# Delta heads: pairwise decays from spread rows of running sums and a minimum, in place of masked copies summed by products

## The chip, the core and the metric

The kernel runs on one core of a Trainium2 chip. A core has a matrix engine (TensorE; PE in the profile, its weight loads PEld), three engines for element work (VectorE, DVE; ScalarE, ACT; GpSimd, POOL) and SyncE (SP), whose queue issues nearly all transfers between the device memory and the on-chip memories. Each engine works through its own list of instructions in a fixed order; an instruction that waits for a semaphore holds up everything behind it on that engine. The metric is the device time of one execution in microseconds (us), the median of several runs.

## What is computed

One layer of a bidirectional encoder trunk over 1024 tokens of width 1024, in float32: a combined input projection, then in parallel a windowed softmax attention and a bidirectional gated delta rule ("delta heads"), an output projection, a cross-attention into 256 memory tokens, and a feed-forward block. The change lies in the delta heads. There are 4 heads and 2 directions; the tokens are cut into chunks, and inside a chunk every pair of tokens has a decay:

```python
g = -exp(a_log) * softplus(a + dt_bias)          # per token, direction and head; negative
g = cumsum(g, within the chunk)
decay = exp(where(i >= j, g[i] - g[j], -inf))    # c x c per chunk, head and direction
lower = where(i > j, (k*beta) @ k.T * decay, 0)  # solved against v and k
qk    = (q @ k.T) * decay
```

The backward direction is the same on reversed tokens. The kernel works with chunks of 128 tokens, 8 of them (NT), and keeps one 128 x 128 table E per chunk and head that serves both directions: above the diagonal it holds the forward decay, below it the backward one. The key products `k.T k` and the query products `k.T q` are multiplied by it.

## The kernel before

The work runs in stages. The first, some 0 to 230 us of the span, normalises x, transposes it and projects it into the q, k and v of the delta heads (`proj`, `gemm_b`, L276: 48 matrix products of 128x128 by 128x512 for each of 12 column tiles, since every float32 operand is split into a high and a low part and three of the four partial products are summed). Beside the projections run a short convolution with SiLU for each tile (`conv`: copies on ScalarE at L298 and L299, four multiply-adds on VectorE at L301, SiLU on ScalarE at L302) and the preparation of the delta heads. The table `ORDER_1` names the steps of this stage in the order in which they are written: `k0 k1 E0 K0 U0 E1 K1 U1 S0 q0 v0 q1 C0 v1 E2 C1 k2 ...`, where a digit is the head. The steps that matter here:

- E, `decays` (L479 ff.): makes the tables E of one head, in two halves of four chunks each.
- K, `turned_keys`: transposes the keys (L459), copies them (L503) and sums their squares (L467, one pass of 128 columns each).
- U, `key_products`: products of keys (L474) into a PSUM bank, times E (L513).
- S, `beta_rows`: one transpose (L450) of a small tile, stored to device memory and read back by `base_inverse`.
- C, `query_products`: products of queries (L474), times E (L521), masked for each direction (L524); then transposes of queries and values (L459).
- B, `base_inverse`: a triangular inverse in 31 small steps on VectorE (L560, L562).

All PSUM tiles of these steps come from one pool of 5 banks (`small()`), so a transpose or a product can start only when an earlier tile of the pool has been read. In `decays` before, the exponent is summed by TensorE. For each half of a head, the per-token logs g are multiplied with a triangular mask into four 128x512 tiles `gm` (two directions, each in a high and a low part, `ghi` and `glo`), and four products with the strict triangles `mU_r`, `mL_r` (L492) add them up in one PSUM bank. The exponential (L495) reads that bank. VectorE makes the masked copies of heads 0 and 1 (L488), ScalarE those of heads 2 and 3 (L491). Nothing in this step goes through device memory.

After the first stage come the remaining levels of the inverse, the window attention and its projections (`ORDER_2`, 230 to 350 us, with `rr` tiles of the pool `ra` for the rotary part), the scan over chunks (`ORDER_3`), and then the output projection, cross-attention and feed-forward, in which the change touches nothing.

The order on each engine isn't the written one: a scheduler with priorities lays the steps out on the engines when the program is built, and fixes there which buffer and which bank each step takes. Weight loads, their casts (L103) and remainders (L104) are written 300 places ahead. A change in one step thus moves others.

## Time and profile before

| what | value |
|---|---|
| time of the runs, median (lowest, highest of 3) | 1501.22 us (1501.08, 1502.55) |
| span of the profiled execution, first to last instruction | 1497.9 us |
| median of the runs less that span | 3.3 us |
| busy in the span: PE, PEld, DVE, ACT, POOL | 98%, 83%, 74%, 52%, 25% |
| mean granted TensorE clock | 0.995 of full speed |
| all tables E made: first masked copy, last exponential | 67.3 us, 170.8 us |

The page has no time for the profiled execution beside its span; the 3.3 us to the median are taken as the part of a run that lies around the span. The row of the page with a share of 98% for PE says how long products were in flight, not that TensorE ran at its peak. Of each line that a view shows, the first numbers are start and duration (in the timeline), or the count and the mean of one (in groups). "idle before" is time in which that engine had nothing to run, and names whom it waited for. Line numbers are those of the kernel before, unless the text says otherwise; in the changed kernel the lines of the first stage are 2 to 7 lower (L457, L472, L499, L465, L509 for L459, L474, L503, L467, L513).

### The profile page before, as it was taken

What the parts mean: (1) busy time and instruction counts of PE and PEld (TensorE: products, weight loads), DVE (VectorE), ACT (ScalarE), POOL (GpSimd) and SP (SyncE); (2) the same over time, 40 slices, a digit from 0 to 9 for tenths busy, and PEclk for the clock granted to TensorE, in tenths of its full rate; (3) what the DMA queues carried; (4) which work ended last, traced back from release to release, by engine and by line L of the source; (5) the groups of instructions that cost most, each with busy time, mean ns of one, the idle gap of its engine ahead of it and who ended that gap; (6) DMA issues with size and microseconds to landing.
All of it is one profiled execution on the core that took longest, in us unless ns stands there. A gap on an engine that the chain in (4) does not pass through costs nothing.

```text
span 1497.9 us, 21340 instructions
## 1 busy us (share of the span) xinstructions
PE 1467.6 (98%) x7437; PEld 1239.1 (83%) x7437; DVE 1108.8 (74%) x1804; ACT 776.3 (52%) x1600; POOL 374.3 (25%) x411
## 2 busy tenths in 40 slices
PE   7999999999999999999999999999999999999998
PEld 6888878888999878888888877888888888888787
DVE  5878998577897866538767887686867774795666
ACT  7678844568567664555554774323223232544533
POOL 0011232442246213342201002343433342000030
PEclk9999999999999999999999999999999999999999
DMA  6244554657996585444855553343533433953355
GB/s 205 71 120 137 142 168 135 168 173 222 297 305 211 158 310 204 163 146 157 277 174 194 183 197 119 121 141 105 168 123 113 138 109 103 351 183 99 105 181 170
DMA packets 254169, 256.35 MB, mean 171 GB/s; under 512 B 18129, under 2 KB 186222, under 8 KB 254062
## 3 DMA queue, kind: packets, MB, share of 16 engines
q1 hardware_dynamic: 252141, 250.80, 52.7%
q0 software_dynamic: 768, 2.10, 0.5%
q10 hardware_dynamic: 1152, 2.10, 0.4%
q8 instruction: 58, 0.95, 0.3%
q14 instruction: 50, 0.40, 0.1%
HBM read 178.63 MB, written 73.70 MB: 168 GB/s over the span
## 4 chain that ended last, share of the span: by engine, by line
PE 73%; DVE 9%; ACT 4%; issue 2%; DMA 2%; SPq 1%; POOL 0%; DVEq 0%; ACTq 0%
PE pE L1511 8%; PE pD L1511 8%; PE pA L1511 6%; PE pmg L1105 6%; PE pcq L276 6%; PE pdX L1733 6%; PE pst L1324 5%; PE pdA L1733 4%; PE pB L1511 4%; PE pg L276 3%; PE psc L844 3%; PE pdD L1733 2%; PE pdX L1842 2%; PE pcs L1195 2%; PE pco L1222 1%
## 5 line engine op out<-in xcount | busy, mean ns | idle before, releaser
L103 ACT CAST whi<-wraw 128x1024 fp32r<-128x1024 f32 x96 | 100.7, 1050 | 119.5 <-DMA wraw<-in_w_gate_up_dram 40.0
L276 PE MATMUL pg<-hlo,whi 128*128 128x512 f32 x352 | 140.5, 399 | 0.0
L276 PE MATMUL pg<-hhi,whi 128*128 128x512 f32 x352 | 139.6, 396 | 0.0
L276 PE MATMUL pg<-hhi,wlo 128*128 128x512 f32 x352 | 139.2, 395 | 0.0
L104 POOL TENSOR_TENSOR wlo<-wraw,whi 128x1024 fp32r<-128x1024 f32 x37 | 90.3, 2440 | 191.1 <-ACT whi L103 179.1
L1511 PE MATMUL pA<-b,whi 128*128 128x512 f32 x352 | 109.7, 393 | 1.9 <-ACT whi L103 1.0
L104 DVE TENSOR_TENSOR wlo<-wraw,whi 128x1024 fp32r<-128x1024 f32 x59 | 72.5, 1228 | 31.1 <-ACT whi L103 27.0
L1511 PEld LDWEIGHTS pA<-b,whi 128*128 128x128 f32 x352 | 65.3, 188 | 17.1 <-ACT whi L103 1.9
L276 PEld LDWEIGHTS pg<-hhi,whi 128*128 128x128 f32 x352 | 66.6, 189 | 13.5 <-ACT hhi L241 0.3
L276 PEld LDWEIGHTS pg<-hlo,whi 128*128 128x128 f32 x352 | 66.8, 190 | 12.6
L276 PEld LDWEIGHTS pg<-hhi,wlo 128*128 128x128 f32 x352 | 66.8, 190 | 12.4
L1733 PE MATMUL pdX<-dhl,whi 128*128 128x512 f32 x264 | 76.1, 390 | 0.9 <-ACT dhl L103 0.7
L1603 POOL TENSOR_TENSOR act<-act,up 128x512 f32<-128x512 f32 x33 | 50.3, 1524 | 88.6 <-DVE up L1602 67.3
L103 ACT CAST whi<-araw 128x1024 fp32r<-128x1024 f32 (+1 forms) x36 | 35.3, 981 | 68.2 <-PE pdX L1733 27.6
L1511 PE MATMUL pA<-b,wlo 128*128 128x512 f32 x176 | 69.0, 392 | 0.5 <-DVE wlo L104 0.5
L104 DVE TENSOR_TENSOR wlo<-araw,whi 128x1024 fp32r<-128x1024 f32 (+1 forms) x36 | 40.8, 1132 | 33.6 <-ACT whi L103 33.5
L1574 POOL TENSOR_TENSOR sr<-wraw 128x512 f32<-128x512 f32 x22 | 30.0, 1363 | 139.1 <-DMA wraw<-in_w_gate_up_dram 87.1
L301 DVE SCALAR_TENSOR_TENSOR acc<-cp,cols,acc 128x1024 f32<-128x1024 f32 x48 | 63.1, 1316 | 0.2
L1733 PEld LDWEIGHTS pdX<-dhl,whi 128*128 128x128 f32 x264 | 49.3, 188 | 12.1 <-ACT dhl L103 1.1
L103 ACT CAST dhl<-b 128x512 fp32r<-128x512 f32 x66 | 40.3, 620 | 31.3 <-PE pdA L1733 13.5
L1575 DVE TENSOR_TENSOR sr<-sr,wraw 128x512 f32<-128x512 f32 x22 | 36.7, 1666 | 26.2 <-POOL sr L1574 26.2
L103 ACT CAST s0h<-sr 128x512 fp32r<-128x512 f32 x22 | 13.7, 622 | 79.1 <-POOL sr L1574 78.8
(504 smaller groups left out, 4331.5 us busy)
## 6 DMA issues: line engine op xcount, KB each, us to landing
wraw<-in_w_gate_up_dram SPq DMA_DIRECT2D x54, 512.0 KB, 3.9
kv<-d_kv SPq DMA_DIRECT2D x32, 512.0 KB, 6.0
wraw<-in_w_in_dram SPq DMA_DIRECT2D x22, 512.0 KB, 4.1
b<-in_w_down_dram SPq DMA_DIRECT2D x20, 512.0 KB, 6.3
araw<-d_as SPq DMA_DIRECT2D x20, 512.0 KB, 3.6
pz<-d_pz SPq DMA_DIRECT2D x32, 256.0 KB, 6.3
wraw<-in_w_ckv_dram SPq DMA_DIRECT2D x16, 512.0 KB, 5.0
wraw<-in_w_out_dram SPq DMA_DIRECT2D x16, 512.0 KB, 5.4
```

The source lines that it names most:

```text
L103: nc.scalar.copy(hi, src)
L104: return (eng or nc.vector).tensor_tensor(lo, src, f32(hi), ALU.subtract)
L276: nc.tensor.matmul(p_, w[:, k, :], ah[a][:, k, :], start=(k == 0 and i == 0), stop=(k == nk - 1 and i == 2))
L301: nc.vector.scalar_tensor_tensor(acc, cp[:, t:t + S], taps[t], acc, ALU.mult, ALU.add)
L844: nc.tensor.matmul(out[:, d, h, :], lt[:, d, h, :], rt[:, d, h, :], start=True, stop=True)
L1105: nc.tensor.matmul(pp[t], act[a][:, k, tt], w_[:, kk, :], start=(k == 0 and i == 0), stop=(k == KT - 1 and i == 2))
L1324: nc.tensor.matmul(bank, a[:, tt], w, start=(start and i == 0), stop=(stop and i == 2), skip_group_check=not check)
L1511: nc.tensor.matmul(out_, w[a][:, k, :], xx[b_][:, k, :], start=(start and k == 0 and i == 0), stop=(k == HK - 1 and i == 2), skip_group_ch ...
L1574: nc.gpsimd.tensor_tensor(s[0], b_[:, 0:HK], b_[:, HK:], ALU.add)
L1575: nc.vector.tensor_tensor(s[1], s[0], a_[:, 0:HK], ALU.subtract)
L1603: nc.gpsimd.tensor_tensor(o_, o_, up, ALU.mult)
L1733: nc.tensor.matmul(banks[t], a[:, k - k0, tt], w, start=(first and k == 0 and i == 0), stop=(k == NB - 1 and i == 2), skip_group_check=not ...
```

## The change

`decays` no longer uses TensorE. The kernel already computed the inclusive running sums of g within a chunk, forward and backward, by a product with triangles (L385), for the small factors EG. The change copies these sums out of PSUM (`sums`, and the backward ones negated, `nsums`), transposes them once to 64 rows of 128 (`sT`), and stores these rows to device memory (`d_sum`, 32 KB). For each half of a head, two transfers read 512 values of a row back and spread them over all 128 partitions (`ahead`, 256 KB each, one for each direction). ScalarE subtracts the token's own backward sum in four pieces of 128 columns (a bias of one value per partition), VectorE subtracts the own forward sum, takes the minimum of the two differences, and ScalarE takes the exponential. Since g is negative, the forward difference is the smaller one above the diagonal and the backward one below it. The tile `ahead` takes the buffers `rr` of the pool `ra`, two of them, which the rotary step uses later.

```diff
+    sums = sm.tile([P, 2, 4, NT], F32, name="sums")
+    nc.vector.tensor_copy(sums, pv[:, 0])
+    nsums = sm.tile([P, 4, NT], F32, name="nsums")
+    nc.vector.tensor_scalar(nsums, sums[:, 1], -1.0, None, ALU.mult)
...
+    pt = small()
+    nc.tensor.transpose(pt[0:64, 0:P], sums.rearrange("p d h c -> p (d h c)"), ident)
+    sT = t1.tile([64, P], F32, tag="sT", name="sT")
+    nc.vector.tensor_copy(sT, pt[0:64, 0:P])
+    nc.sync.dma_start(d_sum, sT)
...
     def decays(h):
 
+        by_row = d_sum.rearrange("(d h c) n -> d h (c n)", d=2, h=4)
         for b in range(2):
-            pa = small()
-            n = 0
-            for d, (mi, ml) in enumerate((("mUi", mL_r), ("mLi", mU_r))):
-                for part in (ghi, glo):
-                    gm = t2.tile([P, 4, P], F32R, tag="gm", name="gm")
-                    if h < 2:
-                        nc.vector.tensor_tensor(gm, bc(part[:, d, h, 4 * b:4 * b + 4], 2, (P, 4, P)), bc(cm[mi], 1, (P, 4, P)),
-                                                ALU.mult)
-                    for j in range(4 if h > 1 else 0):
-                        nc.scalar.activation(gm[:, j, :], cm[mi], AF.Identity, scale=part[:, d, h, 4 * b + j:4 * b + j + 1])
-                    nc.tensor.matmul(pa, ml, gm.rearrange("p c n -> p (c n)"), start=(n == 0), stop=(n == 3))
-                    n += 1
+            c4 = slice(4 * b, 4 * b + 4)
+            ahead = ra.tile([P, 2, HALF], F32, tag="rr", name="ahead", bufs=2)
+            for d in range(2):
+                nc.sync.dma_start(ahead[:, d], by_row[d, h, b * HALF:(b + 1) * HALF].partition_broadcast(P))
+            ahead = ahead.rearrange("p d (c n) -> p d c n", c=4)
             E = Es[h, b] = t2.tile([P, 4, P], F32, tag="E", name="E", bufs=4)
-            nc.scalar.activation(E, pa.rearrange("p (c n) -> p c n", c=4), AF.Exp)
+            for j in range(4):
+                nc.scalar.activation(ahead[:, 1, j], ahead[:, 1, j], AF.Identity, bias=nsums[:, h, 4 * b + j:4 * b + j + 1])
+            nc.vector.tensor_tensor(E, ahead[:, 0], bc(sums[:, 0, h, c4], 2, (P, 4, P)), ALU.subtract)
+            nc.vector.tensor_tensor(E, E, ahead[:, 1], ALU.min)
+            nc.scalar.activation(E, E, AF.Exp)
```

Gone with it are `mU_r`, `mL_r`, `ghi`, `glo` and the five small copies that made them.

The scheduler lays the first stage out anew. On TensorE, where the keys of head 0 are transposed and multiplied, stood before:

```order
L492 MATMUL ps<-gm,mL_r 128x512
L459 MATMUL ps<-ident,acc 128x128 x8
L474 MATMUL ps<-acc 128x128 x3
L492 MATMUL ps<-gm,mL_r 128x512
L474 MATMUL ps<-acc 128x128 x5
```

with further products of L492 between the projection products, every 8 to 14 of them, ahead of these rows and behind them. At the same place there stand in the changed kernel (ps are banks of the pool of 5, here with their numbers; acc_462 and acc_475 are the keys of heads 0 and 1):

```order
L386 MATMUL ps_587<-ident_68,sums_574 64x128
L457 MATMUL ps_654<-ident_68,acc_462 128x128 x4
L457 MATMUL ps_673<-ident_68,acc_462 128x128 x4
L472 MATMUL ps_693<-acc_462 128x128 x4
L472 MATMUL ps_701<-acc_462 128x128 x4
L457 MATMUL ps_730<-ident_68,acc_475 128x128 x4
```

The key products of head 0 (ps_693, ps_701) and, 24 and 36 projection products later, those of head 1 (ps_769, ps_777) now occupy four of the five banks until the tables E have been multiplied into them. Some 60 projection products further on TensorE, the step S of the first two heads and the query products of head 0 follow, and then a transpose:

```order
L448 MATMUL ps_788<-ident_68,bp0_784 32x128
L472 MATMUL ps_1003<-acc_852,acc_462 128x128 x4
L472 MATMUL ps_1016<-acc_852,acc_462 128x128 x4
L457 MATMUL ps_1028<-ident_68,acc_852 128x128 x4
L271 MATMUL pg_1080<-hlo0_152,whi_1076 128x512
```

The bank of ps_1028 is that of ps_769: in the built program this transpose waits for the VectorE product U of head 1, first half, which reads ps_769 and the table E of head 1.

On ScalarE stood before, from the first exponential to the second:

```order
L495 ACT_TABLE_LOAD
L495 ACTIVATE E<-ps 128x512
L298 COPY cp<-pg 128x512
L299 ACTIVATE acc<-pg,cols 128x512
L503 COPY kt<-ps 128x512
L467 ACTIVATE jk,ss_670<-ps 128x128 x2
```

There the exponential waits only for a PSUM bank. In the changed kernel the work from the first table E of head 0 to the first of head 1 (the last row) stands like this; `ahead` is a spread row, L465 squares, L293 and L294 the copies of a convolution, L297 a SiLU:

```order
L491 ACT_TABLE_LOAD
L491 ACTIVATE E<-E 128x512
L465 ACTIVATE jk,ss_757<-ps 128x128 x2
L293 COPY cp<-pg 128x512
L294 ACTIVATE acc<-pg,cols 128x512
L491 ACTIVATE E<-E 128x512
L488 ACTIVATE ahead<-ahead,nsums 128x128 x4
L297 ACT_TABLE_LOAD
L297 ACTIVATE acc<-acc 128x1024
L488 ACTIVATE ahead<-ahead,nsums 128x128 x4
L491 ACT_TABLE_LOAD
L491 ACTIVATE E<-E 128x512
```

Eight pieces of `ahead` and three switches of tables stand in this row, all ahead of the table E on which the transpose above depends. On the whole program the changed order has 24 table loads on ScalarE, the one before 32.

On SP, in the changed kernel, the row store and the spread loads stand between the stores of the turned keys, and one weight load (`wraw`) stands behind them:

```order
L752 DMA d_kv_101<-acc 128x8x128
L389 DMA d_sum<-sT 64x128
L500 DMA d_kv_101<-kt 128x4x128
L484 DMA ahead<-d_sum 128x512 x4
L500 DMA d_kv_101<-kt 128x4x128
L125 DMA wraw<-in_w_in_dram 128x8x128
```

Before, that weight load came directly behind the store `d_kv<-acc`. On all engines the order differs from before up to about 640 us of the span, into the output projection; behind that it is the same.

More of the change, by code (lines that the diff above doesn't have):

```diff
@@ L141, in tile_hybrid_block @@
     C = sm.tile([P, C1 - C0], F32, name="C")
-    mU_r = sm.tile([P, P], F32R, name="mU_r")
-    mL_r = sm.tile([P, P], F32R, name="mL_r")
     prm = sm.tile([P, 24], F32, name="prm")
@@ L187, in tile_hybrid_block @@
     d_u = [dram.tile([2, NT, P, P], F32, name=f"d_u{g}") for g in range(2)]
+    d_sum = dram.tile([2 * 4 * NT, P], F32, name="d_sum")
     d_beta = [dram.tile([32, P], F32, name=f"d_beta{g}") for g in range(2)]
@@ L259, in tile_hybrid_block @@
     nc.sync.dma_start(C, consts[:, C0:C1])
-    with tc.issue_after(scaled.ins):
-        nc.vector.tensor_copy(mU_r, cm["mU"])
-        nc.vector.tensor_copy(mL_r, cm["mL"])
     nc.sync.dma_start(prm[:, 0:8], a_log[0].rearrange("d h -> (d h)").partition_broadcast(P))
@@ L371, in tile_hybrid_block @@
     dump("beta", beta)
-    ghi = sm.tile([P, 2, 4, NT], F32, name="ghi")
-    glo = sm.tile([P, 2, 4, NT], F32, name="glo")
-    ghr = t1.tile([P, 2, 4, NT], F32R, tag="ghr", name="ghr")
-    nc.vector.tensor_copy(ghr, G)
-    nc.vector.tensor_copy(ghi, f32(ghr))
-    nc.vector.tensor_tensor(glo, G, ghi, ALU.subtract)
     pt = small()
```

## The prediction

> **What bounds the kernel now.** First the busy times by stretch (columns: stretch in us, its length, then busy time and count of PE, PEld, DVE, ACT and POOL, granted clock, DMA share, GB/s); the tables E are made between 67 and 171 us:
>
> ```profile
> 60.00:110.00 50.00, 50.00 (x252) 42.35 (x251) 37.69 (x54) 37.38 (x86) 5.18 (x13) 1.00 0.32 91
> 110.00:160.00 50.00, 50.00 (x267) 42.72 (x267) 44.35 (x69) 45.18 (x117) 7.45 (x15) 1.00 0.49 138
> 160.00:210.00 50.00, 50.00 (x263) 42.49 (x262) 46.97 (x75) 28.33 (x97) 10.49 (x15) 1.00 0.54 149
> 210.00:260.00 50.00, 47.52 (x246) 39.35 (x245) 44.53 (x100) 24.49 (x48) 15.87 (x36) 0.97 0.53 150
> 320.00:400.00 80.00, 76.66 (x512) 69.45 (x511) 61.03 (x159) 53.48 (x118) 27.37 (x43) 0.98 0.81 253
> ```
>
> TensorE has no gap from 60 to 210 us: what it is given less there shortens the stage, and what it has to wait for lengthens it. VectorE is close behind (47 of 50 us in the third stretch). Next, whom TensorE waited for at the end of this stage and in the next (total, times, longest), and from the timeline its largest wait among the windows:
>
> ```profile
> PE ptv L808 <- ACT rr L805: 0.7, 1, 0.7
> PE ps L632 <- ACT mov L651: 0.7, 1, 0.7
> PE ps L459 <- ACT acc L302: 0.5, 1, 0.5
> PE ps L632 <- DVE mov L652: 0.3, 1, 0.3
> ...
> 373.25 0.44 PE L685 MATMUL psw<-khi,qs 128*128 128x384 f32 x1 [2.16 <-DVE m L687]
> ```
>
> Then the products that go, and TensorE's pace from its timeline (start, duration):
>
> ```profile
> L492 PE MATMUL ps<-gm,mL_r x16: 389/391/476, 70.2 to 159.3; 128*128 128x512 f32 x16
> L492 PE MATMUL ps<-gm,mU_r x16: 389/389/477, 76.1 to 165.4; 128*128 128x512 f32 x16
> ...
> 68.69 0.48 PE L276 MATMUL pg<-hlo,whi 128*128 128x512 f32 x1
> 81.98 1.03 PE L459 MATMUL ps<-ident,acc 128*128 128x128 f32 x8
> 82.85 0.83 PE L474 MATMUL ps<-acc 128*128 128x128 f32 x6
> 96.02 0.39 PE L276 MATMUL pg<-hhi,whi 128*128 128x512 f32 x1
> 101.91 0.39 PE L276 MATMUL pg<-hhi,whi 128*128 128x512 f32 x1
> ```
>
> Products overlap, so their price is the distance of starts. From 96.02 to 101.91 us there are 26 steps: 0.227 us each, L492 among them. Eight transposes take 82.85 - 81.98 = 0.87, so 0.109 each.
>
> **The change, part by part.**
>
> *TensorE.* 32 products go: 32 x 0.227 = 7.25 us. One transpose comes: +0.11. All of it is on the path, since TensorE has no gap there: -7.14.
>
> *The new chain to E.* It is long, and TensorE meets its end. First TensorE's own walk down the changed order, without waits, from the product at 68.69 (unchanged up to there) to the transpose ps_1028, which needs a bank that U of head 1 reads last: 84 projection products (22 + 18 + 6 + 12 + 26) x 0.227 = 19.0, and 42 transposes and small products x 0.109 = 4.6, so it arrives at 92.3. The chain it waits for is priced by these rows of ScalarE, VectorE and the transfers (last number of a transfer: us from issue to landing):
>
> ```profile
> 75.88 0.36 SPq L756 DMA_DIRECT2D d_kv<-acc  x1
> 78.08 0.37 SPq L125 DMA_DIRECT2D wraw<-in_w_in_dram  x1
> ...
> wraw<-in_w_in_dram SPq DMA_DIRECT2D x22, 512.0 KB, 4.1
> d_kv<-acc SPq DMA_DIRECT2D x8, 512.0 KB, 3.2
> pz<-d_pz SPq DMA_DIRECT2D x32, 256.0 KB, 6.3
> act<-d_a SPq DMA_DIRECT2D x5, 256.0 KB, 2.6
> a<-d_m SPq DMA_DIRECT2D x10, 256.0 KB, 3.9
> mraw<-d_mix SPq DMA_DIRECT2D x4, 512.0 KB, 9.0
> ```
> ```profile
> 74.80 1.06 ACT L302 ACTIVATE acc<-acc 128x1024 f32<-128x1024 f32 x1
> 75.76 1.03 ACT L103 CAST whi<-wraw 128x1024 fp32r<-128x1024 f32 x1
> 82.61 0.58 ACT L503 COPY kt<-ps 128x512 f32<-128x512 f32 x1 [0.80 <-PE ps L459]
> 83.09 0.28 ACT L467 ACTIVATE jk<-ps 128x128 f32<-128x128 f32 x1
> 83.35 0.28 ACT L467 ACTIVATE jk<-ps 128x128 f32<-128x128 f32 x1
> 88.14 1.28 ACT L495 ACT_TABLE_LOAD   x1
> 89.44 0.60 ACT L495 ACTIVATE E<-ps 128x512 f32<-128x512 f32 x1
> 89.93 1.05 ACT L103 CAST whi<-wraw 128x1024 fp32r<-128x1024 f32 x1
> 90.87 0.59 ACT L298 COPY cp<-pg 128x512 f32<-128x512 f32 x1
> 91.34 0.70 ACT L299 ACTIVATE acc<-pg,cols 128x512 f32<-128x512 f32 x1
> 121.92 1.28 ACT L491 ACTIVATE gm<-C,ghi 128x128 fp32r<-128x128 f32 x4 [0.86 <-PE ps L492]
> 123.11 1.27 ACT L491 ACTIVATE gm<-C,glo 128x128 fp32r<-128x128 f32 x4
> ```
> ```profile
> 83.49 1.28 DVE L301 SCALAR_TENSOR_TENSOR acc<-cp,cols,acc 128x1024 f32<-128x1024 f32 x1
> 84.69 0.68 DVE L488 TENSOR_TENSOR gm<-glo,C 128x512 fp32r<-128x512 f32 x1
> 85.29 0.68 DVE L513 TENSOR_TENSOR U<-ps,E 128x512 f32<-128x512 f32 x1
> ```
>
> The transpose of the sums starts at 68.69 + 22 x 0.227 = 73.7, its copy is done at 74.2. On SP a 512 KB store of q goes just ahead; its SiLU (74.80 before) comes about 1.5 earlier, since two masked copies of 0.60 and three small ones ahead of its convolution go, so that store (75.88 before) is issued at about 74.3 and lands 3.2 later; the row store behind it lands with it, at about 77.5. The four spread loads then follow each other at 0.36 to 0.4; ScalarE needs the second, issued at 77.9. Its landing isn't shown before; the nearest rows of its size are 2.6 and 3.9 (reads of 256 KB in rows of 2 KB), the furthest 9.0. I take 3.1: 81.0. From there ScalarE has no wait: up to the end of E of head 1, first half, it has 16 pieces of `ahead` in fours, priced by the masked copies of the same size (123.11 - 121.92 = 1.19 a four): 4.8; 7 squares at 0.26: 1.8; a key copy 0.48; 3 table loads at 1.30: 3.9; 3 exponentials at 0.49: 1.5; two convolution copies 1.06; a SiLU 0.96: together 14.5, so 95.5. U (0.60) ends at 96.2 with its start-up. TensorE stands from 92.3 to 96.2: +3.9 us. Ends: ScalarE itself is busy with key copies and squares until about 80.1, so the chain can't start before, and the wait is at least 3.0; with a landing of 9.0 it is 3.9 + 5.9 = 9.8.
>
> [...]
>
> *ScalarE otherwise.* 64 pieces go and 32 come (-32 x 0.30 = -9.5), and 8 table loads go (-10.4). TensorE never waits for it between 110 and 210 us, so this is worth nothing there. It frees ScalarE, which is what keeps later waits small.
>
> *VectorE.* 16 masked copies go, 8 subtractions and 8 minima of the same size come: 16 x 0.60 both ways; of the small copies five go and three come, all below 0.3. What moves is the time: the eight of heads 2 and 3, before on ScalarE, fall between about 103 and 129 us, among the start of the inverse. Down VectorE's list from U at 96.1 to the last multiply-add of v of head 1 there are 8 multiply-adds (1.20, 84.69 - 83.49), 14 pieces of 0.60, two remainders and the start of the inverse, together about 25: 121.4, its SiLU 122.4. TensorE reaches the transposes of that tile at 121.7: +0.9 with the latency (ends 0 and 2.5, by one multiply-add each way).
>
> *SP and transfers.* One store and 16 loads come, 4.2 MB. The transfer engines are 32 to 49% busy from 60 to 160 us, which covers them. The weight load behind them is issued some 1.5 us later, and has slack: issued at 78.08 before, landed 4.1 later, it was cast at 89.93. If that cover went, TensorE would wait for the weights, microsecond for microsecond.
>
> *Downstream.* TensorE arrives earlier at the levels, and VectorE with it: the query products of head 1 no longer wait for a bank behind the masked copies of head 2. The four waits listed add up to 2.2; I take 1.0 off. Ends: all 2.2 off, or a new one like that at 373 us, 2.2 on, since the order changes up to 640 us.
>
> Sum: -7.14 + 3.9 + 0.9 - 1.0 = -3.3 us on a span of 1497.9, that is 1494.6; with the 3.3 us that the median of the runs lies above this span, 1497.9 us. 0.2%, about what a measurement of this kernel can tell from no change, is 3.0 us: the border to faster lies at 1498.2, just above the forecast.
>
> **The rivals.**
>
> - The wait doesn't arise: the loads land at once and something on ScalarE steps aside, so nearly all 7.1 remain, with the 1.0: 1493 to 1494. Against it stands the 3.0 us lower end. 8%.
> - The lead is given back downstream. The rows at 222, 244 and 373 us show TensorE waiting for VectorE and ScalarE by 0.3 to 2.2; if their chain keeps its time, TensorE waits there for what it has gained: 1501. Against it: VectorE does the query products of head 1 some 20 us earlier. 20%.
> - Slower: the spread loads, 128 reads of the same row behind other transfers, land late. The wait grows one to one; above a landing of 5.4 the first stage gains nothing (-7.1 + 3.9 + 2.3 + 0.9), and at 9.0, with the 1.0 downstream not gained, the sum is -7.1 + 9.8 + 0.9 = +3.6: 1504.8. For it: loads of 256 KB that follow a store to the same place took 6.3 in the scan. Against it: those ran from about 350 us on, with the transfer engines 81% busy in the stretch from 320 us, against 32% here. 24%.
> [...]
>
> **How the numbers follow.** The forecast holds 46%, with its own range of 1495 to 1500.5; about 32 of these lie below 1498.2. Faster: 32 + 8 = 40%. Same: 14 of the forecast, 15 of the second rival, 5 of the third, 2 of the fourth: 36%. Slower: 5 and 19: 24%. The range from 1494 to 1505 takes in the lower end of the wait (-7.1 + 3.0 - 2.2 = -6.3) and the late landing, and leaves out some of the first rival and anything worse than the third.
>
> **What would show it.** Right: no L492; TensorE starts L457 of ps_1028 at 95 to 98 us with an idle time of about 4 us before it, ended by VectorE's U; spread loads landing in 2.6 to 4 us; fours of `ahead` at about 1.2; 24 table loads; the first stage ending about 2 us earlier; the waits at 212 to 244 us smaller. Wrong: a gap of 8 us or more there or a second one of that kind, a wait for weights, or new waits among the levels and windows that together exceed 2 us.

## The result and the profile after

| | kernel before | changed kernel |
|---|---|---|
| median of the runs beside each other | 1501.15 us (4 runs) | 1508.89 us (4 runs, 1507.37 to 1511.05) |
| ratio, with its 95% interval | 1 | 1.0059 (1.0041 to 1.0076) |
| span of the profiled execution, mean granted clock | 1497.9 us, 0.995 | 1506.6 us, 0.992 |

The changed kernel is slower by 0.6%, 7.7 us by the medians. It was forecast at 1497.9 us, with 24% for slower and a range that ended at 1505. The same stretches as in the prediction, now of the changed kernel:

```profile
60.00:110.00 50.00, 46.17 (x243) 38.98 (x242) 34.17 (x52) 40.04 (x118) 7.88 (x14) 0.97 0.54 155
110.00:160.00 50.00, 48.88 (x244) 41.12 (x243) 48.54 (x73) 33.96 (x76) 15.68 (x17) 1.00 0.67 179
160.00:210.00 50.00, 50.00 (x263) 42.66 (x262) 48.22 (x76) 20.60 (x68) 9.45 (x16) 1.00 0.52 139
210.00:260.00 50.00, 48.78 (x256) 41.30 (x255) 41.34 (x96) 23.44 (x47) 17.21 (x37) 0.97 0.54 151
320.00:400.00 80.00, 72.86 (x453) 65.10 (x452) 53.09 (x135) 49.23 (x113) 27.65 (x41) 0.91 0.75 229
```

TensorE has gaps now (46.17 and 48.88 of 50), and from 320 to 400 us it fits in 453 products where it had 512, at a granted clock of 0.91 instead of 0.98. Two lines tell where the time goes: the transposes of the first stage (first and last start at the end of the row), and the first group of the output projection, behind the scan. First of the kernel before, then of the changed one:

```profile
L459 PE MATMUL ps<-ident,acc x96: 270/272/328, 82.0 to 212.8; 128*128 128x128 f32 x96
...
L1105 PE MATMUL pmg<-whi,s0h x64: 389/389/792, 531.5 to 580.4; 128*128 128x512 f32 x64
```
```profile
L457 PE MATMUL ps<-ident,acc x96: 270/273/413, 73.0 to 212.9; 128*128 128x128 f32 x96
...
L1101 PE MATMUL pmg<-whi,s0h x64: 387/389/793, 539.6 to 587.8; 128*128 128x512 f32 x64
```

The first stage ends at the same time, 212.9 for 212.8 us, although 7 us of products have gone. (This execution was 0.9 us early ahead of everything changed, and still is around 172 us. Executions differ by such amounts: with the same first stage, the first of these transposes starts at 73.0 us here and at 74.7 in e1, below. So the length of the stage is taken below between the projection products that start at 65.4 and 172.0 us in the kernel before: 106.6 us there, and 106.6 in the changed kernel.) In the ten profiled executions that have this first stage (the changed kernel's and those of nine of the experiments below) the length differs from 106.6 by -0.3 to +2.3. The output projection starts 8.1 us late in the changed kernel, and the spans are 8.7 apart. So there are two places: a first stage that gains nothing, and a loss between 212 and 540 us, where the change touches no step and only the order is new.

Where in between it is lost shows at the points up to which TensorE has done the same products in both kernels. At 320.7 us of the kernel before the changed kernel is 3.3 us early. At 338.0 it is 1.2 late: half clock lasts from 331.1 to 337.9 there. At 361.4 it is 1.3 late, at 365.8 by 10.1, and at 386.6 by 5.0 again, since in between the kernel before has its own wait of 2.16 us with half clock behind it. From 547 us on it is 7.4 late.

In the first stage TensorE waits as forecast, for U of head 1:

```profile
PE ps L457 <- DVE U L509: 3.1, 1, 3.1
PE ps L457 <- ACT acc L297: 1.1, 1, 1.1
PE ps L448 <- DVE bp L446: 0.7, 1, 0.7
```
```profile
73.90 1.95 PE L472 MATMUL ps<-acc 128*128 128x128 f32 x16
...
98.63 0.80 PE L457 MATMUL ps<-ident,acc 128*128 128x128 f32 x4 [3.08 <-DVE U L509]
...
100.08 0.63 PE L271 MATMUL pg<-hhi,whi 128*128 128x512 f32 x1
100.50 0.63 PE L271 MATMUL pg<-hlo,whi 128*128 128x512 f32 x1
```

The last two rows show what the prediction didn't look for. Behind the wait the products start 0.42 us apart, where they started 0.227 apart ahead of it: TensorE runs at half its clock. By short stretches (the granted clock is the third number from the end):

```profile
98.00:100.00 2.00, 1.37 (x6) 1.26 (x7) 1.75 (x3) 2.00 (x4) 0.00 (x0) 0.75 0.56 202
100.00:102.00 2.00, 2.00 (x6) 1.53 (x5) 2.00 (x4) 1.89 (x7) 0.00 (x0) 0.50 0.81 228
102.00:104.00 2.00, 2.00 (x11) 1.62 (x11) 2.00 (x3) 2.00 (x13) 0.00 (x0) 0.90 1.10 298
...
332.00:336.00 4.00, 4.00 (x11) 3.42 (x12) 2.11 (x6) 0.58 (x1) 0.20 (x1) 0.50 0.31 108
...
364.00:368.00 4.00, 0.50 (x1) 0.19 (x1) 2.41 (x7) 4.00 (x13) 0.00 (x0) 1.00 1.11 299
368.00:372.00 4.00, 2.68 (x13) 2.71 (x13) 4.00 (x6) 1.86 (x4) 2.38 (x1) 0.58 1.09 244
372.00:376.00 4.00, 3.85 (x16) 3.27 (x15) 2.25 (x7) 1.53 (x2) 0.00 (x0) 0.56 1.01 346
```

From 98 to 104 us, 2 x (0.25 + 0.50 + 0.10) = 1.7 us of clock are withheld, that is half clock for 3.4 us. From 368 to 376 it is 4 x (0.42 + 0.44) = 3.4 us, half clock for 6.9. That second one stands behind the largest wait of the changed kernel; from 347 us on TensorE waits for

```profile
PE pow L713 <- ACT ph L103: 4.6, 2, 3.8
PE ptw L708 <- DVE m L683: 1.8, 1, 1.8
PE psc L840 <- DMA kv<-d_kv: 1.7, 1, 1.7
```

The kernel before, behind its wait of 2.16 us at 373:

```profile
372.00:376.00 4.00, 2.75 (x17) 2.75 (x18) 3.20 (x10) 1.35 (x4) 1.32 (x2) 0.85 1.04 401
376.00:380.00 4.00, 4.00 (x27) 3.92 (x26) 0.60 (x3) 3.31 (x10) 0.81 (x2) 0.72 1.03 401
```

4 x (0.15 + 0.28) = 1.7 us withheld, half as much.

### The profile page after: what moved, and what is told of

The parts are those of the page before. It is cut to its first block, busy times and chain, and to the rows that moved or that the text cites. A ratio compares the mean times of both kernels' runs of the same rounds, so it can differ in the third digit from the quotient of the medians.

```text
span 1506.6 us, 21280 instructions
## 1 busy us (share of the span) xinstructions
PE 1465.9 (97%) x7406; PEld 1237.0 (82%) x7406; DVE 1104.0 (73%) x1802; ACT 757.7 (50%) x1560; POOL 386.3 (26%) x411
## 4 chain that ended last, share of the span: by engine, by line
PE 68%; DVE 10%; DMA 6%; ACT 3%; issue 2%; SPq 1%; POOL 0%; DVEq 0%; ACTq 0%; POOLq 0%
PE pE L1507 7%; PE pD L1507 7%; PE pmg L1101 6%; PE pcq L271 6%; PE pdX L1729 6%; PE pg L271 5%; PE pA L1507 5%; PE pst L1320 5%; PE pB L1507 3%; PE pdA L1729 2%; PE psc L840 2%; PE pdD L1729 2%; PE pdX L1838 2%; PE pcs L1191 2%; PE pco L1218 1%
## 5 line engine op out<-in xcount | busy, mean ns | idle before, releaser
L271 PEld LDWEIGHTS pg<-hhi,wlo 128*128 128x128 f32 x352 | 67.2, 191 | 13.1
L103 ACT CAST dhl<-b 128x512 fp32r<-128x512 f32 x66 | 40.3, 619 | 31.2 <-PE pdA L1729 13.3
L1507 PE MATMUL pB<-s0h,s1h 128*128 128x512 f32 x176 | 54.2, 389 | 0.0
```

The costliest lines, as they stand in the source:

```text
L103: nc.scalar.copy(hi, src)
L271: nc.tensor.matmul(p_, w[:, k, :], ah[a][:, k, :], start=(k == 0 and i == 0), stop=(k == nk - 1 and i == 2))
L1507: nc.tensor.matmul(out_, w[a][:, k, :], xx[b_][:, k, :], start=(start and k == 0 and i == 0), stop=(k == HK - 1 and i == 2), skip_group_ch ...
```

## Experiments

They ran on several chips, each beside the kernel before; ratios are to that one and are what should be compared between experiments. Many experiments hold the order of instructions fixed. The scheduler lays all steps out anew when one step changes, so the changed kernel differs from the kernel before in its tables E and in the order of some 1,400 of TensorE's 6,061 instructions behind the first stage, up to 640 us. A table of positions in the written program, one list for each engine, is applied when the program is built and separates the two; it adds order, no work and no wait for an end:

```diff
+    for table in LAID_OUT.values():
...
+        for one, nxt in zip(row, row[1:]):
...
+            tc.add_manual_dep(nxt, one.name,
+                              mybir.DependencyInfo(mybir.DependencyClass.NoSync, mybir.DependencyReason.DATA),
+                              reason="laid_out_as")
...
     L0.close()
+    laid_out_as(tc, first_stage_ends)
```

### Tables or order

`e1_after_old_order` is the changed kernel with the old order behind the first stage, `e2_before_new_order` the kernel before with the new one.

> The changed kernel, whole, but every instruction written behind the first stage stands on its engine in the order that it has in the kernel before (a table pins the order; no work is added or left out). Order theory: what was lost between 347 and 628 us comes from the new order of windows and scan alone; it goes, TensorE's wait of 3.8 us before L713 and the slow clock behind it go too, and the time is 1497 to 1501, with products of the output projection starting within 2 us of the kernel before. Rival (the new tables themselves, their transfers and the earlier arrival of the first stage, cost the time later): still 1507 to 1511, and the loss between 347 and 628 stays 8 us or more. Both: the first stage ends as in the changed kernel, its wait of about 3 us near 96 us unchanged.

> The kernel before, whole, but everything written behind the first stage in the order of the changed kernel. Order theory: slower by 6 to 11 us, 1507 to 1512, lost between 320 and 640 us, with a wait of 3 us or more for ScalarE or VectorE in the windows around 365 us. Rival (the new tables cost it): within 3 us of 1501.

Measured: e1 1500.45 us, ratio 0.9994 (0.9979 to 1.0010); e2 1505.37, ratio 1.0033 (1.0019 to 1.0048). The start of the output projection, of e1 and then of e2:

```profile
L1127 PE MATMUL pmg<-whi,s0h x64: 387/389/499, 531.9 to 579.5; 128*128 128x512 f32 x64
```
```profile
L1131 PE MATMUL pmg<-whi,s0h x64: 387/389/500, 536.8 to 583.9; 128*128 128x512 f32 x64
```

In the old order the changed kernel is back at the time of the kernel before, with the wait near 96 us unchanged; in the new order the kernel before loses 5 us without any change to its tables (a little less than the 6 that theory wanted), with the waits that theory named (3.8 us for the cast near 367 us, 2.0 for kv behind it). So the order makes most of the loss. The new tables as such are worth nothing that can be told in the old order. In the new one the changed kernel takes some 3.5 us more than e2; the intervals of the two ratios overlap, and what makes this part isn't shown.

### Why the first stage gains nothing

`e3_fewer_products` takes 24 of the 32 products L492 off TensorE in the kernel before, all orders pinned; of each four partial sums of the exponent it leaves out three:

```diff
-                    nc.tensor.matmul(pa, ml, gm.rearrange("p c n -> p (c n)"), start=(n == 0), stop=(n == 3))
+                    if n == 0:
+                        nc.tensor.matmul(pa, ml, gm.rearrange("p c n -> p (c n)"), start=True, stop=True)
```

> The kernel before without 24 of its 32 products L492 (of each four only the first is left, so the exponents are wrong; the masked copies stay), every engine's order otherwise as before, to the end. Prediction's term for TensorE: 24 x 0.227 = 5.4 us less at the end of the first stage (products L276 around 200 us start 5.4 us earlier), and the time falls by 4 to 6, to about 1496. Rival (VectorE, or the transfers, set the pace of the first stage, so what TensorE saves is waited away before 220 us): the stage ends less than 2 us earlier and the time falls by less than 2.

Measured: 1501.12 us, ratio 1.0004 (0.9991 to 1.0018). The rival is right. New waits of TensorE from 60 to 215 us:

```profile
PE ps L484 <- ACT jk L492: 1.6, 1, 1.6
PE ps L484 <- ACT acc L327: 0.7, 1, 0.7
PE ps L499 <- ACT E L521: 0.7, 2, 0.5
PE ps L499 <- ACT jk L492: 0.5, 1, 0.5
```

3.5 of the 5.4 us come back as waits for ScalarE, which still makes masked copies here; the stage is 1.3 us shorter. And a wait of 2.6 us at 267 us, with half clock behind it (0.50 from 270 to 275 us), took what was left in the profiled execution. That TensorE has no gap didn't mean that it alone set the pace.

`e4_no_round_trip` lets the spread loads read a constant (first diff), `e5_gap_filled` is e1 with 11 projection products moved on TensorE ahead of the four transposes that wait (second diff, of its order):

```diff
-                nc.sync.dma_start(ahead[:, d], by_row[d, h, b * HALF:(b + 1) * HALF].partition_broadcast(P))
+                nc.sync.dma_start(ahead[:, d], consts[16 * d + 4 * b + h, 0:HALF].partition_broadcast(P))
...
-            nc.scalar.activation(E, E, AF.Exp)
+            nc.scalar.activation(E, E, AF.Exp, scale=1e-4)
```
```diff
+L271 MATMUL pg 128x512 x11
 L457 MATMUL ps_1028 128x128 x4
-L271 MATMUL pg 128x512 x11
```

> The changed kernel with everything behind the first stage in the order of the kernel before, and the 16 spread loads read rows of a constant input instead of the sums, so that they needn't wait for the store of the sums (exponents are then wrong and scaled by 1e-4; number, size and form of the transfers and all work on ScalarE and VectorE stay). If the round trip through device memory makes the wait near 96 us: the first four loads come before the sums are ready, the wait of 3.1 us and the half clock behind it go, and the first stage ends 4 to 6 us earlier than in the changed kernel. If ScalarE's own chain (pieces, squares, table loads) makes it: the wait stays above 2 us, and the stage ends within 2 us of the changed kernel's.

> The changed kernel, whole, behind the first stage in the order of the kernel before (as in e1_after_old_order), and in the first stage one move: on TensorE the 11 projection products that stand behind the four transposes ps_1028 go ahead of them, so that they run while U of head 1 is awaited. Clock theory: the wait of 3.1 us in e1 cost its own length and then about 1.9 us more, because the granted clock was 0.5 behind it; filled with 2.5 us of products, the wait shrinks to under 1 us, the clock stays at 1.00 from 94 to 106 us, and the first stage ends 4 to 4.5 us earlier than in e1: time near 1496. Without such a cost: the stage ends 2.5 us earlier at most, time near 1498. If another wait takes its place (VectorE or ScalarE late anyway): less than 1.5 us gained by the end of the stage, time 1499 to 1500.5.

Measured: e4 1496.66 us, ratio 0.9970 (0.9954 to 0.9985), the wait of 3.1 us and the half clock behind it gone (1.00 from 94 to 110 us), the stage 2.8 us shorter than in the changed kernel, between the two theories. So the round trip makes that wait, but the 7 us can't be had without it either. e5 gained nothing: 1500.48, ratio 1.0006 (0.9992 to 1.0019), and in the profiled execution its stage is 4.2 us longer than in the kernel before. The first fence is e1, the second e5:

```profile
98.00:102.00 4.00, 1.24 (x5) 1.25 (x6) 2.44 (x3) 3.97 (x7) 0.00 (x0) 0.70 0.74 190
102.00:106.00 4.00, 4.00 (x11) 3.03 (x10) 4.00 (x6) 4.00 (x18) 0.00 (x0) 0.50 0.93 254
```
```profile
98.00:102.00 4.00, 2.70 (x13) 1.70 (x11) 2.50 (x4) 3.99 (x6) 0.00 (x0) 1.00 0.78 181
102.00:106.00 4.00, 2.54 (x18) 2.33 (x19) 4.00 (x6) 3.79 (x19) 0.00 (x0) 1.00 1.00 272
...
126.00:130.00 4.00, 0.97 (x5) 0.47 (x3) 4.00 (x9) 3.97 (x16) 2.10 (x1) 0.87 0.46 131
130.00:134.00 4.00, 3.25 (x12) 2.96 (x13) 3.29 (x7) 3.98 (x9) 1.87 (x4) 0.50 0.58 158
```
```profile
130.75 1.97 PE L482 MATMUL ps<-ident,acc 128*128 128x128 f32 x8 [3.78 <-ACT acc L322]
```

The clock theory is right at its place (1.00 from 98 to 106 us with the wait filled, 0.5 without), and the rival is right about the time: TensorE arrives earlier at the tile of v that VectorE and ScalarE finish, waits 3.78 us there, and loses the clock there. VectorE is the likely reason. It is a list that runs in order, and the new subtractions stand in it and wait for transfers while multiply-adds of the convolutions, long ready, stand behind them. Its waits in the changed kernel from 66 to 172 us, and the landing of the spread loads:

```profile
DVE E L489 <- DMA ahead<-d_sum: 5.3, 4, 3.0
...
DVE E L490 <- ACT ahead L488: 2.0, 1, 2.0
```
```profile
DMA to landing us min/median/max: 4.0/4.9/5.7
```

After these waits VectorE has hardly any slack from 99 to 131 us (busy for 31.55 of 32), and TensorE meets it at 128.

Two edits try that. `e9_fused` shortens the work (e1's order behind the stage), `e10_late_key_products` writes the queries and values of head 0 ahead of U, `e11_fused_late` does both:

```diff
-            for j in range(4):
-                nc.scalar.activation(ahead[:, 1, j], ahead[:, 1, j], AF.Identity, bias=nsums[:, h, 4 * b + j:4 * b + j + 1])
-            nc.vector.tensor_tensor(E, ahead[:, 0], bc(sums[:, 0, h, c4], 2, (P, 4, P)), ALU.subtract)
-            nc.vector.tensor_tensor(E, E, ahead[:, 1], ALU.min)
-            nc.scalar.activation(E, E, AF.Exp)
+            for j in range(4):
+                c = slice(4 * b + j, 4 * b + j + 1)
+                nc.vector.scalar_tensor_tensor(E[:, j], ahead[:, 1, j], gaps[:, h, c], ahead[:, 0, j], ALU.add, ALU.min)
+            for j in range(4):
+                c = slice(4 * b + j, 4 * b + j + 1)
+                nc.scalar.activation(E[:, j], E[:, j], AF.Exp, bias=nsums[:, h, c])
```
```diff
-k0 k1 E0 K0 U0 E1 K1 U1 S0 q0 v0 q1 C0 v1 E2 C1
+k0 k1 E0 K0 q0 E1 K1 U0 v0 U1 S0 q1 C0 v1 E2 C1
```

(`gaps` is the forward less the backward sum, `nsums` here the forward one, negated.)

> Behind the first stage the order of the kernel before, as in e1_after_old_order; the tables E by a shorter chain: VectorE makes min(ahead1 + gap, ahead0) in one instruction per chunk of 128 columns (the gap of both sums is a scalar per partition), ScalarE takes the exponential per chunk with the own sum as its bias. For a half of a head VectorE then has 4 short instructions for 2 of 0.6 us, and ScalarE 4 pieces for 5. Theory (VectorE and ScalarE set the pace of the first stage in the changed kernel, because the chain to E stands in their lists): the stage ends 2 to 4 us earlier than in e1, and the time falls to 1496 to 1498.5. Rival (only the round trip through device memory counts): the wait near 96 us stays at 3 us, the stage ends within 1 us of e1's, time 1500.

> The changed kernel with the order of the kernel before behind the first stage, and the first stage written in another order: queries of head 0 ahead of U of head 0, values of head 0 ahead of U of head 1, so that more products lie between the sums and the first work that needs E. If TensorE's early meeting with U is the cause: no wait above 1 us near 96, the stage ends 3 to 5 us earlier than in e1, time 1496. If VectorE's list sets the pace: the wait moves to a later place (SiLU of a tile, an exponential), the stage ends within 1.5 us of e1's, time 1499 to 1501.

> e9_fused and e10_late_key_products together. If both chains count: better than either, 1494 to 1496. If VectorE alone: as e9_fused.

Measured: e9 1499.89 us (1.0004, 0.9991 to 1.0016), the stage 2.2 us shorter than in the kernel before, the wait for U 2.3; e10 1500.27 (1.0008, 0.9996 to 1.0021), the stage unchanged, the wait for U still 3.2; e11 1497.05 (0.9987, 0.9975 to 1.0000), the stage 4.5 us shorter, no wait above 1.0. In the stage, moving TensorE's steps alone is worth nothing, a shorter chain 2.2, and both together 4.5: the chain through VectorE and ScalarE limits first, and once it is shorter the order of TensorE's steps is worth as much again. In time and stage, e10 came out as its rival said; e9 missed its theory, since the 2.2 us don't show in it, and e11's 1497.05 lies above the 1494 to 1496 expected. By its ratio e11 is 0.7% below the changed kernel; against the kernel before it is at the border of what can be told.

### Where the new order loses

`e6_kv_loads_ahead` and `e7_casts_ahead` undo what stands at the two waits of the changed kernel near 367 us, `e8_both_moves` both. On ScalarE the changed kernel has the next window's exponentials, with their table load, ahead of the cast that TensorE awaits (first fence); in the kernel before they stand behind it:

```profile
361.40 1.28 ACT L690 ACT_TABLE_LOAD   x1
362.69 0.62 ACT L690 ACTIVATE sc<-sc,nm 128x384 f32<-128x384 f32 x1
...
366.53 0.58 ACT L103 CAST ph<-ptw 128x512 fp32r<-128x512 f32 x1
```
```profile
361.72 0.60 ACT L103 CAST ph<-ptw 128x512 fp32r<-128x512 f32 x1
...
363.32 1.28 ACT L698 ACT_TABLE_LOAD   x1
```

```diff
+kv<-d_kv x2
 kraw<-d_k
 wraw<-in_w_ckv_dram
-kv<-d_kv x2
```
```diff
+ph<-ptw x2
 sc<-sc,nm x4
 mT<-ptm,cols x4
-ph<-ptw x2
```

The first diff is SP's order (e6), the second ScalarE's (e7); on VectorE the remainders pl go ahead of mT likewise.

> The changed kernel in its own order, and behind the first stage one move: on SP two loads of kv for the scan go ahead of kraw and the weight load, where the kernel before has them. If the late kv loads are what costs 10 us from 347 us on: the time falls by 4 us or more, to about 1504. If the wait for the cast ph (3.8 us, ScalarE) holds TensorE there anyway: the wait of 1.7 us for kv goes, that for ph stays, and the time falls by 1 to 2, to about 1507. If neither: no change, 1509.

> The changed kernel in its own order, and behind the first stage one move on two engines: the two casts ph on ScalarE go ahead of the next window's four exponentials, and their remainders pl on VectorE ahead of the memory norm's multiply-adds, as in the kernel before. If the cast is what costs: the wait of 3.8 us before L713 goes, and with it part of the slow clock, time 1503 to 1505. If the kv loads hold TensorE right behind it: the wait moves to kv (3 us or more there), and the time stays at 1507 to 1509.

> Both moves of e6_kv_loads_ahead and e7_casts_ahead. If these two places carry the loss behind 347 us: no wait above 1.5 us and no clock below 0.8 between 360 and 376, the lead at the end of the scan improves by 5 to 9 us, time 1500 to 1504. If the loss is spread over the whole new order: at most 3 us better, 1506 to 1509.

Measured: 1505.66, 1509.37 and 1506.52 us (ratios 1.0036, 1.0053, 1.0046). With the loads ahead the wait for kv goes, and 3 us or so with it, more than its 1.7 and less than the theory of the late loads wanted. With the casts ahead nothing is gained (1509.37 with a table, 1508.89 for the changed kernel without one: no cost of the table itself shows), since TensorE then waits at the same place for the memory norm's multiply-adds on VectorE; from 347 to 400 us of e7:

```profile
PE psc L866 <- DVE mT L131: 5.5, 1, 5.5
```

Neither move takes the loss away, and both together don't: e8 came out as the theory of a loss spread over the whole order said. `e13_new_to_300`, `e14_new_to_345` and `e15_new_to_378` keep the new order up to a time and go on in the old one:

> The changed kernel, whole; on every engine what has started by 300 us in the changed kernel keeps its new order, and everything later that lies behind the first stage follows in the order of the kernel before. If the loss comes from the order of what runs after 300 us: it goes, and the 2 to 3 us by which the new order leads at 300 us stay: 1496 to 1500. If it was laid earlier: 1505 or more.

> The same with the border at 345 us. If the costly turn lies behind 345 us, as e6 to e8 point to (loads of kv, casts, memory norm): 1497 to 1501, as e13_new_to_300. If it lies between 300 and 345: 1505 or more.

> The same with the border at 378 us. If the loss is made between 345 and 378 us (wait of 3.8 and 1.7 us and the slow clock in the changed kernel): 1505 to 1509. If it builds up in the scan behind 378: below 1502.

Measured: 1504.21 (1.0019, 1.0006 to 1.0031), 1502.26 (1.0018, 1.0004 to 1.0032) and 1507.50 (1.0049, 1.0034 to 1.0063); with the border at 0 it is e1's 1500.45, without one 1508.89. The largest step, 5 us, lies between 345 and 378, as e15 was to show. But e13 and e14 are 2 to 4 us above e1, which their theory didn't allow: in their profiles a wait of 1.24 us near 262 us has half clock for 6.83 us behind it, which e1's has not, and by equal products e13 loses 5.4 us against e1 between 260 and 272 us. The changed kernel's first profile has no such stretch near 262 us, its second one (e18) has; so how much of the loss this place makes in the mean is left open.

Is the order worth something by itself? `e12_fused_free` is e9 without a table, `e16_both_best` is e11 with the order that e12 was given:

> e9_fused with nothing pinned, in the order that the scheduler gives it. Order theory: behind 347 us it resembles that of the changed kernel, so 5 to 9 us above e9_fused, 1502 to 1507. If the order behind the first stage is not what costs: within 2 us of e9_fused.

> The first stage of e11_fused_late, and behind it the order of e12_fused_free, which led by 3 us more up to 347 us and lost 3.3 behind. If the lead of the first stage (4.5 us) and the gains of each order add up: 1494 to 1496, below the kernel before by 0.2% or more. If the order is only worth something with the first stage it was made for: 1498 to 1501.

Measured: e12 1498.41 (0.9984, 0.9972 to 0.9996), e16 1499.16 (0.9997, 0.9985 to 1.0008). Both times the theory missed and its rival came true: e12 is within 2 us of e9, and e16 lies between 1498 and 1501. The scheduler's free order, with the same wait of 3.7 us for the cast in it, isn't slower than the pinned old one here, and under another first stage it shows no gain. So the scheduler's own order costs 5 to 9 us in one program and nothing in a neighbour, and a wait for the cast doesn't by itself make a kernel slow.

### The clock

Each run reports its mean granted clock. Means over the runs; the last column is the time at full clock, were all withheld clock lost:

| kernel | runs | time | clock | time x (1 - clock) | time x clock |
|---|---|---|---|---|---|
| before, beside the experiments | 139 | 1500.1 | 0.9975 | 3.7 | 1496.4 |
| changed, both sets of runs | 10 | 1509.2 | 0.9913 | 13.1 | 1496.1 |
| e1, old order | 12 | 1500.0 | 0.9954 | 6.9 | 1493.2 |
| e2, before in the new order | 12 | 1505.8 | 0.9953 | 7.0 | 1498.8 |
| e4, no round trip | 10 | 1496.6 | 0.9971 | 4.3 | 1492.2 |
| e11, fused and late | 12 | 1497.2 | 0.9962 | 5.6 | 1491.6 |
| e12, fused, free order | 10 | 1497.5 | 0.9937 | 9.4 | 1488.1 |

(In each profile the last stretch at half clock, some 3 to 7 us, lies behind the last product and costs nothing; that part is in every row.) By this table the changed kernel loses nothing but clock: 9.1 us more time, 9.4 us more of it withheld. It isn't so for every pair: e2 is 5.7 us slower with 3.3 more withheld, and e12 is faster than the kernel before with 5.7 more, so an order also moves the time at full clock. And a table shows only that both go together. `e17_idle_products` tests which makes which: it adds work to TensorE and changes nothing else.

```diff
         po = pw.tile([P, 4, P], F32, tag="pow", name="pow", bufs=1)
+        for _ in range(14 if (n, g) == (3, 0) else 0):
+            nc.tensor.matmul(po.rearrange("p h t -> p (h t)"), vhl[:, k0, g].rearrange("p r e -> p (r e)"),
+                             keys[g][0][:, 0:512], start=True, stop=True)
```

> The changed kernel in its own order, with 14 products more on TensorE and nothing else: they stand ahead of the product that waits 3.8 us for the cast ph near 367 us, read operands that are long ready, and their result is overwritten by that product (none of the computation is left out). They fill some 3.2 us of that wait. Clock theory (the slow clock for 6.83 us behind the wait costs 3.4 us on top of the wait): the wait shrinks to below 1 us, the clock at 0.5 behind 368 us goes or falls to 3.41 us, and the kernel gets faster with more work: 2 to 4 us below e18_changed_again. If the wait alone costs: no difference (within 1 us), since the cast comes when it came.

> The changed kernel once more, beside the kernel before. All theories: 1507 to 1510, 0.4 to 0.6% over the kernel before, with stretches of clock 0.5 behind waits near 99, 242, 331, 368 and 539 us; each lasts 3.4 or 6.8 us. If these stretches are chance alone, other ones than these appear.

Measured on the same chip: e18 1509.53 us (ratio 1.0055, 1.0040 to 1.0070), e17 1504.73 (1.0029, 1.0017 to 1.0041). Fourteen products more make the kernel 4.8 us faster. The first fence is e18, the second and third e17:

```profile
368.00:372.00 4.00, 0.71 (x1) 0.20 (x1) 2.40 (x7) 4.00 (x13) 0.00 (x0) 0.91 1.08 298
372.00:376.00 4.00, 3.13 (x14) 3.06 (x15) 4.00 (x6) 1.87 (x4) 2.38 (x1) 0.50 1.08 269
```
```profile
368.00:372.00 4.00, 2.84 (x21) 2.59 (x21) 4.00 (x7) 1.75 (x4) 2.39 (x1) 1.00 1.07 266
372.00:376.00 4.00, 1.97 (x10) 1.44 (x9) 2.96 (x8) 1.53 (x2) 0.00 (x0) 0.91 1.02 384
```
```profile
362.98 3.46 PE L731 MATMUL pow<-khi,vhl 128*128 128x512 f32 x14
367.04 0.50 PE L741 MATMUL pow<-ph,vhl 128*128 128x512 f32 x1 [0.60 <-ACT ph L128]
```

The cast comes when it came (367.04 for 367.16 in the changed kernel's profile), the wait that is left is 0.60, and the work behind it runs at full clock up to 375.3 us. The withheld clock falls from 13.3 to 8.5 us by the runs' means, and the mean time by 4.8, so that the time at full clock is the same, 1496.0: what the idle products bring is clock. Where they bring it, the profile doesn't settle. Against the changed kernel's first profile e17 is level up to 367 us and 2.3 us early at 375, but TensorE then waits 1.6 us for the next cast ph, the next stretch at half clock follows, and by 380 the lead is gone; the 3.3 us by which e17 leads from 545 on come between 415 and 440 us and near 540, where this execution has no half clock and the other has. That some of the 4.8 comes from such chance isn't excluded.

In e18 the stretches of half clock among the products stand near 129, 265, 337, 371 and 1494 us; of the five places named in advance only those at 331 and 368 come again (it runs some 3 us later there). In the changed kernel's first profile they begin at 99.00, 242.36, 331.11, 368.66 and 539.32 us and last 3.41 us, those at 331 and 368 6.83. Which of the shorter waits is hit changes from one execution to the next, and the length of a wait alone doesn't tell it: in that first profile waits of 0.94 and 0.28 us, before products that start at 239.81 and 241.16, have half clock behind them, and one of 1.12 us, before a transpose at 128.03, has not (granted clock 1.00 from 110 to 160 us). The wait for U there, 3.08 us, ends at 98.63, and half clock follows from 99.00 on. In e18 it is as long, and none does; what decides it isn't shown:

```profile
99.61 0.65 PE L457 MATMUL ps<-ident,acc 128*128 128x128 f32 x4 [3.09 <-DVE U L509]
...
94.00:106.00 12.00, 8.44 (x53) 7.41 (x54) 8.51 (x13) 11.96 (x33) 0.20 (x1) 1.00 0.74 200
```

## Why the prediction was wrong

The step that failed is the sum itself: it had no term for the clock, and its term downstream, -1.0 with ends of 2.2 either way, was far too small for an order that is new over 400 us.

- **The clock: the term that was missing.** Every wait stood in the sum with its length alone. The wait of 3.08 us near 98 cost 1.7 more behind it, the one at 367 another 3.4; over the whole run 9.4 us more are withheld than before, as much as the loss. The row for it was in the prediction (0.98 for 320 to 400 us, 0.97 for 210 to 260) and wasn't read as the price of a wait. Beside the 35 runs of the kernel before on its own chip (mean 1501.0 us, 4.5 withheld), e1 is 3.3 us faster at full clock, the -3.3 of the sum, and 2.4 of it are withheld again. No run has full clock throughout, so that agreement is a calculation and may be luck.
- **Downstream, -1.0 with ends of 2.2 either way: the term that was mis-sized.** Up to 320 us the relief came: the changed kernel was 3.3 early, 2.4 of it won behind the first stage, a little more than the good end of the term. From there to the output projection the same kernel loses 10.7. The prediction named the sign that came true ("new waits in the levels and windows that together exceed 2 us") and quoted the wait at 373 us as the pattern, but bounded a new order by the waits of the old one. e2 shows that the order alone is worth 5 us, e17 that 4.8 us of the changed kernel's time are clock. Rival two, the lead given back downstream, had the right place and the wrong size: 1501.
- **TensorE, -7.14: right as a count, wrong as time.** The stage that lost these products ended 0.1 us later. In the changed kernel the terms beside it took the time back: TensorE waits 4.9 us there (3.1, 1.1 and 0.7) and loses 1.7 of clock, together 6.6. But the step from "no gap" to "all of it is on the path" failed by itself too: in the kernel before, 24 products less brought 1.3 of 5.4 us (e3). A busy share of 50 of 50 was read as a bound without asking how close VectorE (47 of 50) and ScalarE (45) were behind.
- **The wait, +3.9: right by luck, by errors that cancel.** It was 3.08, and 0.74 for bp before it that the sum didn't have: 3.8. TensorE arrived at 95.6, not 92.3, although this execution was 0.9 early: the order lists a key product once, the trace shows two passes for each (16 records for 8 rows), and the walk of 24 of them left out 24 x 0.11 = 2.6. U came at 98.6, not 96.2. Half of that is the loads, which landed in 4.9 us, not 3.1, so that ScalarE's first piece started at 82.2 instead of 81.0; the other half is its own list, in which a later load held it up by 0.45. The bound of 9.0 wasn't reached, nor the 5.4 from which the third rival lived. That rival had the right sign for a reason that didn't occur.
- **VectorE crowding, +0.9: 1.1 measured**, and 2.4 in e18, but as the second bound, not as a residue: with the first wait filled it is 3.8 (e5).
- **ScalarE, and SP and transfers, at nothing.** Right in the first stage: TensorE waited for no weights. On SP it failed later: two loads of kv, issued at 354 us before, stand behind a load that is held up until 361.5; with them ahead the wait of 1.7 goes and the time falls by some 3 us (e6).
- **Table loads.** 24, as forecast. On the new chain the exponential starts 1.29 us after its load, which itself takes 1.28, so the price of 1.30 in the sum held:

```profile
86.61 1.28 ACT L491 ACT_TABLE_LOAD   x1
87.90 0.64 ACT L491 ACTIVATE E<-E 128x512 f32<-128x512 f32 x1
```

What bore on this case was the half clock, in stretches of 3.41 and 6.83 us. 2.16 us of waiting was enough for it (before, at 373 us: granted clock 0.50 from 374.81 to 378.22), and so was a wait of 1.24 us, with 0.5 more right behind it (e13, e14).

## What to carry to other kernels

Price a wait of TensorE of some 1 to 4 us at its length plus what half clock took behind such waits here, 1.7 us (behind 2.16 and 3.08 us) or 3.4 us (behind 3.8), as a chance, since the wait of 3.09 us in e18 had none behind it; and if it can't be avoided, try to fill it with products whose result is thrown away: that bought 4.8 us in the mean for 14 products here. When a change makes the scheduler lay out the steps behind it anew, measure it once with the old order pinned: by their ratios the change itself was worth -0.9 us, within the noise, and the new order +5 us alone (e2) and some +9 together with the change. And a share of 50 of 50 on one engine is worth taking work off only down to the next engine's list, in which a new instruction that waits for a transfer holds up what stands behind it (VectorE waited 5.3 us in all for the spread loads).

## What was not expected of the hardware

- TensorE's clock falls to half in stretches of 3.41 or 6.83 us behind waits of 2 to 4 us (2.16 in the kernel before, 3.08 and 3.8 in the changed one), and at waits near 1 us among small products (0.94 and 0.28 us among 128x64 outputs near 241 us, 0.21 and 0.84 by 128x32 outputs near 331 us: granted clock 0.50 from 332 to 336). A wait of 3.09 us (e18) and one of 1.12 (changed kernel, at 128 us) had none behind them; what decides it isn't shown. Executions of one kernel differ: e14's runs went from 1499.14 us at a clock of 0.996 to 1509.89 at 0.990.
- Fourteen products more on TensorE made the kernel 4.8 us faster in the mean (e17 for e18).
- A spread load of 256 KB, one row of 2 KB read for each of 128 partitions, landed in 4.0 to 5.7 us (transfer share 0.54 from 60 to 110 us). In the kernel before, other loads of its size took 2.6, 3.9 and, at a share of 0.81, 6.3.
